# A hybrid decoder block on one core: one pool of 90 tiles in place of four pools, and a new written order

## The chip, the cores and the metric

The kernel runs on one core of one Trainium2 chip. The metric is the device time of one execution in microseconds (us). Five engines work side by side: PE (TensorE, the matmuls), DVE (VectorE), ACT (ScalarE), POOL (GpSimd) and SP (SyncE). SP and POOL compute nothing here: SP issues the loads and stores, POOL issues the DMAs that add into a tile on chip. "L284" is line 284 of the kernel.

## The reference, cut to what matters

One decoder layer on x of 512 tokens by 1024 columns, f32, with D_FF = 2816:

```python
mod = silu(c) @ ada_w + ada_b
shift1, scale1, gate1, shift2, scale2, gate2 = split(mod, 6)
h = rmsnorm(x, norm1_w) * (1 + scale1) + shift1
proj = h @ w_in                              # one projection, split into 14 column groups
...                                          # conv4 and silu on q, k, v
o_g = gated_delta_chunked(q_g, k_g, v_g, log_decay, beta)   # 4 heads, chunks of 64, triangular solve
o_g = rmsnorm(o_g, gdn_out_norm_w) * silu(gz)
o_n = nsa_attention(q_n, k_cmp, v_cmp, k_slc, vsl, k_win, vwn, gates)   # 4 heads, 3 branches
x = x + gate1 * (concatenate([o_g, o_n]) @ w_out)
h2 = rmsnorm(x, norm2_w) * (1 + scale2) + shift2
a, b = split(causal_dwconv(h2 @ ffn_w_up, ffn_conv_w, ffn_conv_b), 2)
x = x + gate2 * ((silu(a) * b) @ ffn_w_down)
```

## The kernel before, in words

**Products.** Every f32 product is made of three matmuls on fp32r halves. `split` (L337) rounds a tile to its high half with a copy on ACT or DVE and takes the low half with a subtraction on DVE; `split_acc` (L341) writes minus the high half on ACT or DVE and lets a POOL DMA add the source to it (`accum_op`), which spares DVE. The up and the down projection of the MLP use a seven-product scheme on 256-token halves (`pair`, L1211, and L1285 to L1370): sums and differences of weight blocks are formed by DVE adds and by more accumulating DMAs on POOL.

**Stages.** The modulation vectors (`adat`, column sums on DVE, L459), the first projection columns (`g0`), the convolution and the chunked delta rule of four heads, the compressed, selected and sliding attention, the output projection, the gates (`gate_b`, L932 to L936, which loads `adag`), the up projection (`wu`) and the down projection (`wd`). The triangular solve goes through DRAM: blocks are stored to `du`, stepped through on DVE in 64 rows, stored to `dx`, and loaded back as four tiles.

**Order.** The Python code only records operations: `_Plan.record` (L234) appends each one, `either` records one that may run on ACT or on DVE. `ORDER` and `CHOICE` are packed tables; `order()` (L247) gives the one order in which all operations are written and the engine of each `either`. Within each engine the instructions run in that order, each as soon as its inputs are there. SP's queue is such an order too: a DMA whose tile slot is not yet free holds up every DMA written behind it.

**Slots.** `emit` (L257) gives a tile its slot when its first operation is written: the slot that has been free the longest in its class. It is handed back after the operation written last on that tile. What is loaded into a slot therefore waits for that earlier tile's last reader. The classes (L295): S 74 tiles of 512 columns, W 8 (high and low halves of weights), R 4 of 1024 (weights as they are loaded), A 4 (the `adat` and `adag` loads), s 32 small ones, P the 8 PSUM banks. C holds tiles that stay for the whole run, each at its own place: parameters `pt`, constants `ct` (1219 columns), `ident`, the state `St`. All instructions of the plan are issued in `emit`, so their line is L284. A warm-up of 59 matmuls on the identity precedes the work.

Of the kernel before, what the change touches and what calls it, by code (L numbers as in the profile page):

```python
# [62 lines left out]
c-oy?cbrV;*FWdZ%r-  # L63
<>y@cpi?<H6wT1W&xf&|e8Nwg?I)C36<L??v=(S_)%{Se6#qIc1ITWp)T&w0PkbMK6m*Za@=na|GLd!Ksx_nhZ$6b<o?@{9@iJ(H3WB|74MQgafqh~3X
p@lrebMe5Kt2_sMF`TzIxiusPhUoN^S%cKoil%M_-r!^bRqF%UOEJ|8adh+ACB0Z4%@>B{^I9-
v4l9|rnX*~*~1Gs)H|CRrHwKr+Kr2Tt~*5U7tJeJaQNa{x%OgbtBD4Om|26}>d(qqgMDM=@!KAn=Q@&)}QNfMBkC|UfVKOJ2Z8yv|*8PGE){wBDq52Ab
0((o%umYZjT>9*uU|8$ffg}~ErJPV^oas#a%d=zGS89eYyidk7dsYQpyZ`#ADB%Q;U#}bKEGooKOJ(Zi1A1!{#O7p<Ei;|HVfeYbg2R^J9j@Emi=mz%C
i)`%pka^~OB0)t_$g(|VWL*Cxg8MAAovSFOBiKz2x+|Hm$4Jt9Qqq@}$R*LVdg!4<({*{BPD>2tKPOLcA47F%x7-
mA_TNf|Q7v#U3_UZ@HH<$mwP}x(r2=$Ge&ymS2Aocj2&zPJatouMNO5qwB<OevyUvDnbAgHkDF%HQM9aXJ3{*+BnbnKaJnD>9>xRcCI~>o5{dp)+j$+>
)DnUtdPoglMK?74h`W^ecF6A)mdU?-  # L70
# [1443 lines left out]
```

## Time and profile before

| | before |
|---|---|
| three runs, us | 665.75, 666.3, 668.78 (median 666.3) |
| profiled execution: its own time, us | 668.34 |
| profiled execution: span, us | 666.6 |
| instructions in the profile | 12647 |
| matmul records | 4177 |
| mean granted TensorE clock | 0.997 |
| DMA, MB | 129.39 |

The profile is of one execution, whose span begins with its first instruction; 1.7 us of its time lie around the span. All times inside the run are counted from the start of the span. PE is the TensorE matmul stream, PEld its weight loads, which run beside it. In a row of the timeline "[0.98 <-DVE S]" means that the engine stood idle for 0.98 us just before, and that an instruction of DVE that wrote an S tile ended the wait. "S<-dx" is a load from the DRAM tensor `dx` into an S tile; SPq and POOLq are the DMA-issuing parts of SP and POOL. The granted clock is at full speed in the whole run, so it plays no part below.

### The profile page before, as it was taken

The numbers are of one execution on the slowest core, as the hardware profiler recorded it, in microseconds if no ns is written. First come the engines' busy times: TensorE is split into PE (matmuls) and PEld (weight loads), VectorE is DVE, ScalarE is ACT, GpSimd is POOL, SyncE is SP. The second block draws the span as 40 slices with busy tenths as digits, with TensorE's granted clock in tenths as the row PEclk, the third lists the DMA queues.
The fourth block names the chain that finished last, engine by engine and source line by source line (L and its number), as shares of the span: only waits on it lengthen the run. The fifth ranks groups of instructions, "written<-read, shape, count | busy, mean of one in ns | idle before, by whom it ended". The sixth has DMA issues, their size and how long they took to land.

```text
span 666.6 us, 12647 instructions
## 1 busy us (share of the span) xinstructions
PE 655.7 (98%) x4177; PEld 586.0 (88%) x4177; DVE 627.6 (94%) x1541; ACT 464.9 (70%) x1157; POOL 126.9 (19%) x148
## 2 busy tenths in 40 slices
PE   8999999999999999999999999999999999999997
PEld 8887788888888878888999999999999997877885
DVE  7999999997899999889999999988999998999997
ACT  7655895645579999656786557576668788987740
POOL 0000000111000004300123244323333432245100
PEclk9999999999999999999999999999999999999999
DMA  9985436666652659965877799898999999999703
GB/s 322 392 306 187 170 134 211 196 158 130 219 162 76 215 176 227 220 198 155 252 175 160 181 181 218 165 198 161 196 224 197 217 233 250 220 217 201 141 0 127
DMA packets 65321, 129.39 MB, mean 194 GB/s; under 512 B 11092, under 2 KB 11620, under 8 KB 65256
## 3 DMA queue, kind: packets, MB, share of 16 engines
q1 hardware_dynamic: 44632, 91.07, 40.7%
q0 software_dynamic: 20624, 37.52, 34.2%
q8 instruction: 33, 0.54, 0.3%
q14 instruction: 32, 0.26, 0.1%
HBM read 108.11 MB, written 3.41 MB: 167 GB/s over the span
## 4 chain that ended last, share of the span: by engine, by line
PE 79%; DMA 8%; DVE 6%; ACT 4%; issue 2%; SPq 1%; ACTq 0%; DVEq 0%
PE P L284 79%; DVE S L284 4%; DMA S<-in_wd_dram 4%; ACT S L284 3%; DMA R<-in_wu_dram 2%; ACT W L284 1%; DVE W L284 1%; DMA S<-in_adat_dram 1%; DMA A<-in_adat_dram 1%; DMA S<-dx 1%; SPq L284 1%; DVE s L284 0%; ACT R L284 0%; ACTq L284 0%; DVEq L284 0%
## 5 line engine op out<-in xcount | busy, mean ns | idle before, releaser
L284 PE MATMUL P<-S,W 128*128 128x256 f32 (+1 forms) x2037 | 304.2, 302 | 1.6 <-ACT S L284 1.0
L284 PEld LDWEIGHTS P<-S,W 128*128 128x128 f32 x2037 | 272.3, 191 | 15.6 <-ACT S L284 1.6
L284 PE MATMUL P<-W,S 128*128 128x512 f32 (+2 forms) x722 | 188.1, 395 | 0.7 <-DVE W L284 0.5
L284 PE MATMUL P<-S,S 128*128 128x512 f32 (+4 forms) x864 | 175.8, 323 | 1.3 <-DVE S L284 1.3
L284 PEld LDWEIGHTS P<-W,S 128*128 128x128 f32 (+1 forms) x722 | 131.0, 186 | 29.1 <-DVE W L284 2.4
L284 PEld LDWEIGHTS P<-S,S 128*128 128x128 f32 (+2 forms) x864 | 132.6, 188 | 16.8 <-ACT S L284 1.4
L284 DVE TENSOR_TENSOR S<-S,S 128x256 fp32r<-128x256 f32 (+16 forms) x318 | 140.9, 474 | 4.8 <-ACT S L284 1.5
L284 ACT ACTIVATE W<-S 128x512 fp32r<-128x512 f32 x149 | 91.4, 625 | 38.9 <-PE P L284 26.1
L284 ACT ACTIVATE S<-P 128x256 f32<-128x256 f32 (+5 forms) x200 | 78.9, 419 | 50.2 <-PE P L284 47.3
L284 DVE TENSOR_TENSOR W<-S,W 128x512 fp32r<-128x512 f32 x155 | 104.5, 684 | 6.3 <-ACT W L284 3.7
L284 ACT ACTIVATE S<-S 128x256 fp32r<-128x256 f32 (+3 forms) x198 | 91.0, 491 | 27.8 <-DVE S L284 22.6
L284 POOL DMA_DIRECT2D S<-R x45 | 41.8, 1016 | 306.3 <-ACT S L284 200.9
L284 ACT ACTIVATE W<-R 128x512 fp32r<-128x512 f32 (+2 forms) x115 | 64.4, 575 | 27.6 <-PE P L284 23.0
L284 POOL DMA_DIRECT2D S<-in_wu_dram x63 | 56.8, 937 | 136.2 <-DVE W L284 125.0
L284 DVE TENSOR_TENSOR S<-P,S 128x256 f32<-128x256 f32 (+3 forms) x116 | 60.7, 528 | 4.1 <-ACT S L284 1.8
L284 DVE SCALAR_TENSOR_TENSOR S<-S,C,S 128x511 f32<-128x511 f32 (+1 forms) x84 | 62.3, 745 | 1.1 <-ACT S L284 0.5
L284 DVE TENSOR_TENSOR W<-R,W 128x512 fp32r<-128x512 f32 (+2 forms) x103 | 59.6, 590 | 1.1 <-PE P L284 0.6
L284 PE MATMUL P<-C,S 128*128 128x128 f32 (+3 forms) x345 | 56.5, 272 | 0.4 <-DMA S<-in_adat_dram 0.3
L284 PEld LDWEIGHTS P<-C,S 128*128 128x128 f32 (+2 forms) x345 | 43.8, 155 | 7.9 <-ACT S L284 1.0
L284 ACT ACTIVATE S<-S,C 128x512 f32<-128x512 f32 (+1 forms) x63 | 42.0, 675 | 7.0 <-DVE S L284 6.2
L284 ACT ACTIVATE S<-S,s 128x128 f32<-128x128 f32 (+4 forms) x78 | 36.3, 485 | 1.1 <-PE P L284 0.5
L284 ACT ACTIVATE S<-R 128x512 fp32r<-128x512 f32 x48 | 29.4, 627 | 10.5 <-DMA R<-in_wu_dram 5.8
(96 smaller groups left out, 502.7 us busy)
## 6 DMA issues: line engine op xcount, KB each, us to landing
S<-in_wu_dram POOLq DMA_DIRECT2D x63, 256.0 KB, 5.2
R<-in_wu_dram SPq DMA_DIRECT2D x23, 512.0 KB
S<-R POOLq DMA_DIRECT2D x45, 256.0 KB, 5.1
S<-in_wu_dram SPq DMA_DIRECT2D x42, 256.0 KB
S<-in_wd_dram SPq DMA_DIRECT2D x40, 256.0 KB
S<-in_adat_dram SPq DMA_DIRECT2D x32, 256.0 KB
A<-in_adag_dram SPq DMA_DIRECT2D x32, 256.0 KB
A<-in_adat_dram SPq DMA_DIRECT2D x32, 256.0 KB
```

The source lines that it names most:

```text
L284: getattr(engines[eng], method)(*map(place, args), **{k: place(v) for k, v in kw.items()})
```

## The change

**One pool.** W and A disappear; their tiles come from S, which grows from 74 to 90. The constants `ct` become three S tiles of 512 columns, loaded by three DMAs in place of one, and `St` becomes an S tile, so their slots can be handed on when they are last read. 74 + 8 + 4 + 3 + 1 = 90, so the space on chip is the same but for the 317 columns by which three tiles exceed the constants. R, s, P and the other C tiles stay. In the constants' layout "bd", "row0" and "win" move behind "cmask", so that no constant straddles two tiles.

**New tables.** `ORDER` and `CHOICE` are new. The operations are the same but for the two more DMAs of the constants: 3985 written for PE, 1476 for DVE, 1016 for ACT and 144 for POOL in both, and 321 DMAs on SP before, 323 after. 90 `either` operations go from ACT to DVE and 90 the other way. ACT's table loads, which are put in where its function changes, go from 7 to 11. Matmuls and weight loads that wait on a semaphore: 751 before, 625 after.

Where rows are shown, a name is the tile's class, its number in the plan and, behind the underscore, the number of the instruction in the written program at which the tile is first used. Tile numbers are higher by 2 after the change, because of the three `ct` tiles: S440 before is S442 after. What stands in brackets are the semaphores that the instruction waits for.

First place: SP's queue around the loads that bring the solved blocks back from `dx` (S386, S411, S469, S440 before). Before:

```order
L284 DMA dx_82<-S384_91 64x512 [waits DVE_49]
L284 DMA A705_2021<-in_adat_dram 128x512 [waits DMAHW1_49,DVE_49]
L284 DMA A716_2028<-in_adat_dram 128x512 [waits DMAHW2_49,DVE_49]
L284 DMA S386_2036<-dx_82 128x4x32 [waits DMAHW6_49,DMAHW3_49,DMAHW0_49]
L284 DMA A727_2040<-in_adat_dram 128x512 [waits DMAHW4_49,DVE_49]
L284 DMA S411_2055<-dx_82 128x4x32 [waits DMAHW5_49,DVE_49,PE_49]
L284 DMA S469_2088<-dx_82 128x4x32 [waits DMAHW3_49,DVE_49]
L284 DMA A718_2116<-in_adat_dram 128x512 [waits DMAHW7_49]
L284 DMA S440_2162<-dx_82 128x4x32 [waits DVE_49]
L284 DMA A784_2228<-in_adat_dram 128x512 [waits DMAHW1_49]
```

The same place of SP's queue after the change (S388, S413, S471, S442):

```order
L281 DMA dx_76<-S386_83 64x512 [waits DMAHW1_49,DVE_49]
L281 DMA S388_1977<-dx_76 128x4x32 [waits DMAHW3_49,DMAHW2_49,DMAHW1_49]
L281 DMA S781_1982<-in_adat_dram 128x512 [waits DVE_49]
L281 DMA S751_1989<-in_adat_dram 128x512 [waits DMAHW4_49,DVE_49]
L281 DMA S413_2015<-dx_76 128x4x32 [waits DMAHW5_49,DVE_49]
L281 DMA S471_2027<-dx_76 128x4x32 [waits DMAHW7_49,DMAHW6_49,DVE_49]
L281 DMA S442_2045<-dx_76 128x4x32 [waits PE_49,Activation_49]
```

The four loads now stand within 69 instructions of each other (1977 to 2045) where they stood within 127 (2036 to 2162), and the last of them is written ahead of the `adat` loads that it stood behind.

DVE's rows around the reader of the fourth of these tiles. Before, the reader is the row that names S440, the product with a mask:

```order
L284 TENSOR_TENSOR S470_2150<-S469_2088,C1_874 128x512
L284 TENSOR_TENSOR S395_2169<-P394_2154,C1_874 128x512
L284 TENSOR_TENSOR S441_2173<-S440_2162,C1_874 128x512
L284 TENSOR_SCALAR S521_2159<-S521_2159,s530_2083 128x128
L284 TENSOR_TENSOR S415_2179<-P414_2125,C1_874 128x512
```

After, it is the row that names S442:

```order
L281 TENSOR_TENSOR C332_2166<-C331_1392,C306_1471 128x16
L281 SCALAR_TENSOR_TENSOR s532_2136<-s533_2138,s532_2136 128x16
L281 SCALAR_TENSOR_TENSOR s533_2138<-s532_2136 128x16
L281 TENSOR_TENSOR S443_2173<-S442_2045,S4_1051 128x512
L281 TENSOR_TENSOR s533_2138<-s533_2138,s531_2134 128x16
L281 SCALAR_TENSOR_TENSOR S708_2178,s706_2177<-S707_1313,S17_221 128x512
```

The reader's own tile is first used at instruction 2173 in both programs; the load stood 11 instructions ahead of it (2162) and now stands 128 ahead (2045).

Second place: SP's queue where the loads of the down weights begin. Before:

```order
L284 DMA R1650_7281<-in_wu_dram 128x1024 [waits DMAHW4_49,DMASW1_49]
L284 DMA S1652_7290<-in_wu_dram 128x512 [waits DMASW2_49,DMAHW5_49,DVE_49,Activation_49]
L284 DMA R1984_7434<-in_wd_dram 128x1024 [waits DMAHW6_49,DMASW5_49,DVE_49]
L284 DMA S1805_7474<-in_wd_dram 128x512 [waits DMAHW7_49,DMASW2_49,DVE_49]
L284 DMA S1723_7536<-in_wd_dram 128x512 [waits DMAHW0_49,PE_49]
L284 DMA S1735_7542<-in_wd_dram 128x512 [waits DMAHW1_49,PE_49]
L284 DMA S1809_7563<-in_wd_dram 128x512 [waits DMAHW2_49,PE_49]
L284 DMA S1719_7593<-in_wd_dram 128x512 [waits DMAHW3_49,DVE_49,Activation_49]
L284 DMA S1743_7595<-in_wd_dram 128x512 [waits DMASW5_49,DMAHW4_49,DVE_49,Activation_49]
```

After:

```order
L281 DMA R1652_7236<-in_wu_dram 128x1024 [waits DMAHW7_49,DMASW2_49,DVE_49]
L281 DMA S1725_7261<-in_wd_dram 128x512 [waits DMAHW0_49,PE_49]
L281 DMA S1737_7282<-in_wd_dram 128x512 [waits DMAHW1_49,PE_49]
L281 DMA R1986_7417<-in_wd_dram 128x1024 [waits DMASW6_49,DMAHW2_49,DVE_49,Activation_49]
L281 DMA S1771_7424<-in_wd_dram 128x512 [waits DMAHW3_49,PE_49]
L281 DMA S1721_7428<-in_wd_dram 128x512 [waits DMAHW4_49,PE_49]
L281 DMA S1729_7575<-in_wd_dram 128x512 [waits DMAHW5_49,DMASW5_49,DVE_49]
L281 DMA S1807_7579<-in_wd_dram 128x512 [waits DMAHW6_49,PE_49]
L281 DMA S1733_7581<-in_wd_dram 128x512 [waits DMAHW7_49,PE_49]
```

The first loads of `wd` stand further ahead: S1723 moves from instruction 7536 to 7261 (as S1725) and S1719 from 7593 to 7428 (as S1721), while the add that reads S1723 first is row 1215 of DVE before and row 1214 after.

The diff, cut to its core (of the tables one line each, the whole of the rest but for repeated edits of one form):

```diff
-NCST = _fill(CST, [("triu", 128), ("ones", 128), ("negT", 128), ("neg", 128),
-                   ("lv", 2 * 128), ("bd", 4), ("eye16", 256), ("cmask", 4 * 32), ("row0", 1), ("win", 2 * NCMP)])
+NCST = _fill(CST, [("triu", 128), ("ones", 128), ("negT", 128), ("neg", 128), ("lv", 2 * 128), ("eye16", 256),
+                   ("cmask", 4 * 32), ("bd", 4), ("row0", 1), ("win", 2 * NCMP)])
...
-c-oy?cbrV;*FWdZ%r-
+c-oD72bdJa^LEwD-t7gBbYzYoASW3_kerktQKDi%5F{xeAQBAtBcli+DCs~Xi6Ek64iH6@=pi{MNK}w~z=hqJuK(LTd&{9d&-
...
-    sizes = {"S": (74, 512), "W": (8, 512), "R": (4, 1024), "A": (4, 512), "s": (32, 32), "P": (8, 512)}
-    pools = {c: ctx.enter_context(tc.tile_pool(name=f"p_{c}", bufs=1)) for c in ("C", "S", "W", "R", "A", "s")}
+    sizes = {"S": (90, 512), "R": (4, 1024), "s": (32, 32), "P": (8, 512)}
+    pools = {c: ctx.enter_context(tc.tile_pool(name=f"p_{c}", bufs=1)) for c in ("C", "S", "R", "s")}
...
-    def load_w(src, cls="W", acc=False):
+    def load_w(src, acc=False):
...
-            hi, lo = plan.tile(cls, (P, m), F32R, "w"), plan.tile("S" if acc else cls, (P, m), F32R, "w")
+            hi, lo = (plan.tile("S", (P, m), F32R, "w") for _ in range(2))
...
-    pt, ct, ident = keep("pt", NPAR), keep("ct", NCST), keep("ident", P)
+    pt, ident = keep("pt", NPAR), keep("ident", P)
+    ct = [u("ct") for _ in range(3)]
...
-        return ct[:, at + a:at + a + (m - a if n is None else n)]
+        return ct[at // 512][:, at % 512 + a:at % 512 + a + (m - a if n is None else n)]
...
-            raw = plan.tile("S" if i < 2 else "A", (P, 512))
+            raw = plan.tile("S", (P, 512))
...
-    Q.dma_start(ct, cst)
+    for i, c in enumerate(ct):
+        Q.dma_start(c[:, :min(512, NCST - 512 * i)], cst[:, 512 * i:min(NCST, 512 * i + 512)])
...
-    St = keep("St", 512)
+    St = u("St")
...
-                raw = plan.tile("A", (P, 512))
+                raw = plan.tile("S", (P, 512))
...
-        w = plan.tile("W", (P, 512), F32R, "w"), u("wl", F32R) if acc else plan.tile("W", (P, 512), F32R, "w")
+        w = plan.tile("S", (P, 512), F32R, "w"), u("wl", F32R) if acc else plan.tile("S", (P, 512), F32R, "w")
```

More of the change, by code (lines that the diff above doesn't have):

```diff
@@ new lines @@
+Xq1?Ci{RcXf4jg}1tUV<_Ms<9uWfblwd{Qw#c9+LJ|JNoQhw)<{q~(M{PZ&*AAyi7;>f|2`GNcctj4FcrYv-
+{$uVd5xw^Pr8k#s8F5H<vsMXO8#F|J5z2tB;`=Qv*A*IcSsSsC#6xk5$#9Q7+l|_?YLf&ob)K|6CcG<Je`v`DoQ=+P0`$)m3y)eckSsLjQIxc?t;b{DN
+lcjBZcUyY!k1H>AaMomuaD7N)9~b#5YwIqD2qGQ+{fU>voxxjr);wO8iuu{FH%TCFkW4Pzgv;yzxUGHkHTkHI$u_7?kIwD-ua%z{3Uf<p&>$bW4={4xT
+lY+~B7eBoq)mel1f!MPt<I;K)bEL8k+*x6#6nF^-
+j5n9Ca&ha(q7_xKn^Pzt0`fNXH*qL;n$I6Z`Wn+`}7TrbFX(vAv~$T@k4($Npo30w<PH`$DtD@^Oash+P4X-
+J!;5!x)|XVgU*C^PAfq=BpQC{4hqm|`eX{sgy7x#$;ZO_gXT?hit`Q5b0g>cwFOm<r+gCNyq8B%(+Agv_P-XtNPKT$Q@?qcp*|7-MBaF+cq-
@@ new lines @@
+Nsff8t(dN7uAx%xPQvD9AZDIblpY|*y&~->gt$zgra4o)dppKttRrU%CKhyPlDfhzQ2RpAlVc*$@hzFar;@f5o=-
+)i@yj|v~yFk+tS+MMA{GP>@@Y6U7dn%32V1ggqMgOOHS%Yy<M#(Pg*6d({4^W1S>aMC__yv9bNLmLM<9<Fbn36d#NaR%oJySM3>+~OXCg9k*T|olDHCP
+(v`h#9cwz!w2nmUqz&D|Oznh5Fx9kj({5QWb-
+1WpgiMp&Le`bgJZkS))H*Fw4KjfA@fjdBR4wakAOL;0AKWRPE=!GPsbTp+G0EN+=tOPpE$&{F?t<2RC6-
+m)@o4VhT51~R96YLi(GxNX&@29z(!8=|Jd4KgX!WNo#|ZnVB(AE?Sp(#4WEHVQst~yIYWjUD=*VH~Me{t#-
+tTCXu$^0=|N2%HXDd&&TTn(Y)@b9y*6(hreM4qC?_(sxkqe|qW$UOL#w%88_<p)QO68#;Qb20Rqapm2VA=Gln;5EbT<+M3YPwXkHp)<EC3jIJtn;qcbh
@@ new lines @@
+b{pBh@6%Z<ST4#=|mwXmyrVRE#UDoT{+#)xCMP`U`WE-
+$JBw3tObliS`n&>x@BtXuTkP{NJW!ik{znRv94YfcpceiFldPL8%Iiu7KRzSnJ#qT!hN<6^y^RwL*4CX-MESm%(*{^^q)sj#s8-
+*2T!BK$r*INwD<q&{tRbR0>csH%Gm?>Ht5gR&ghItiLdhq0y32kY96p^E~yFjI%bmcM<b7DsP79(o}7<dPoJ8DL=^*K!aODo-
+r>te*>)@E=<>4hc5zOkEfon>{Mx^T3H+1gP>5w%!g&ND2CVGt=_Ubt9v0kepAK*D^yb}t$4|+{FZ|}%A!OS2h21aqq!sXLvygpjf0ihs-
+2~Mj^f>}MqNMCO}8*gwRC@HTUkWbQ*u*XmZx~8Dg(>7$wf^JyYBuW?V)XLa9^C(OR6-
+4R?kMhlIHH`v+z<o=!LL1JHs9lUmvkNxWxDdjqNJaPSohb^?4&5b`DD%=Ch<KWiL_9wJiYU91=a=-
@@ new lines @@
+r!>0$OJIbH3T=kMTyat)a9eLd?&#!X?J&ihtL8UIR=tkI}rWj?ed5u5NPcO@9FOG6Wb(AN#X_Qk^k&`Wv=hQH3po--
+&@DYwm;Y8I>ZXuho=xs>zM_BtS(B#6tP=rS|SI{2s-k=gv+&Uo^bk&ujW;MrWYWOHcVpVbLf|1opr-
+(0x^_oB@os+1ku%dWK<e0M{!b6lZQ7?^Cr3Q7;YYNKZ3DDun^c%G3o|Kkcu(i6*+tzXGkVLDwI#Pr4ZpLS<q~)pwFH?Gy{Wy<&AU&bqB>njvyFl=5`+d
+xBB-tiY@o=?9Or@MG?b>PEC}-q?3Gx@|tQav+>ARj`4V+9Pkoz!ImlWiB+XBsuBuXK2S;%H{Q!9?5fix5R%*E3Vo)~Q5+eZz|*j9@-
+56x%?V%YbxLM`(pWwh|cL4#A!A}=SwZjOuA03Sa`Yq*`#Qe2?^271=fVhbo71J}8zyIG<85qSL*Shl9Vj@rmN+7M_O5mbLtg7}z?-
+yh;`=Jkm06{)fu#y1gmQ_`KtOVkH^Qkw8gDS;l>n@p;euO(V-
@@ new lines @@
+xisyAZ?U*KY_bBqfm|u4$pUrmz7rln-%XK;xb~M0CRe%tsV7>87gGsX&|aAuJv8ktyqypomEPF2t7>YkrjLzmF3>@4<2DM-
+U1MPTB<S2>Q`QxFqSszlA@9hdUIZ<CsJld7%+}|c(1`0&ZQQMmZkq-NMptlO8v5P?(t7D1sLEUMI1d!zs0iKxYV~FK12vHEm@H|s(UGjrJ7#6SsM)oNr
+|Z-
+ZoUIL)7NY~I8?<Yjyf1H=wco#iA`gV}b?BX(hp&EH^d7(oZObZ&rx@y|!hM{VKcbj=r0aW6=9m2A)1yp{Te1RWAEf^##Z2k+aH|Wrn;A90v}(eq<QJJt
+)0DS2h)5KbRj+n>O?r=JnSIB9W6gMEZ83;x?X=dSP2KdLalMi5?I9kO-
+{gjPxF7+#m|%E#L+?;U)uG<$9*r_)cMd3$Ced5rdHY<|;OSC<kEzdT4(_WP+h_U$GOCK0eoH*PxGS7(E$VkX)q^cOh4{NlRbU-
+m?{oX8(I%6zbAP4r)hsF?O^jWBY-$YS40mR>x$A?HdooS*idzFjoP~zJYf?-
@@ new lines @@
+07@W;!Z*HIA;YBkNC9lv(VY9CpN7qd3OO<z__dBFvnDQO}ko0L$8IbK!V2(o2yh29%UIS9zrZfs-SZZnTYJuYhm^TZEX-
+0Sko;Ldsef1ulyO5{KSBQ=AG*Fh%O}u{=-
+>RIZUP7k%FtBjEY4b4+@XyRREsNw;()%$Uy?gFqt8<ucQO*lX|H9Z(u`suv$;%o;s#}yt9%l~a`?W)*+6(C4n(`yBQB}AOG<~MbM^<{8%AjPse_=)s|J
+Rwbog3C>wbsm${@hm6p(`UYB5AB2vd+*W-
+fLC}Tl(u|{N!(&F%@&!#q9iEGi`cFVIC*irjJU+2lViOSrHs$R)U`)2R77O^xEzac?5pxgmpni0Bal!kMo+F*VemGM~t_dB)il*R0GJeDXoxiOsz^hOO
+itM7eI#_hgxnk@0ytVg+P1#q&Qzt+JhE{O*IMaD|nx^>N8NOFCU>5RPF)$StWf#qtdGsDKZGwF_XPayaRbVgD>D$$D<CILvKHp&5D4&{|!+pO=67=a>(
@@ new lines @@
+#g#QFur_(%rC3ma%#XuRX+08eH$8W)A`s_zLn1N@<FK9P(;lqt!?`J3v5&Gp}`-
+7%4(SB!@xcNw)aP1L1ieP)e$&TuYv2;xfHnvU${|PhE8?p9HJLjkab*1`bjIydcII=FABWDJyio_#$_l!?^aW3f~rVQ+V85Izym$ym_F|%$7ut#LhVZS
+lTP;jbJHmJV4dac2yyqj!TN8>PazaDQ5@u>+D^4T?qPkBM&qTCw4E%>Sv$QtnT=voyMyVWCm&Hdd*26-
+Iml!`>v*gB090Opw6d?<X&h5GZ0(DXH7qjLb_QeJ2Tf>#xmk)@8g=fGS_WUQhpgHg9M(*BnJmN0gXS74_xaH$6&k@uwlwbp<d+Hju&U0JC5gUNL+#gG&
+odw<Qw;QHC^GER#tI$@>*!dztm2LJMjOA`S|T~9+M5*vhbjY0Bm&7#0dF=<vs_pElg=2!^YHke%TQ#h*Cn4m>CJbPhmEyv+}963Pmni^E$0+(7vLjE;X
@@ new lines @@
+yoOFLACj3)lRK9s{y*FBFMSY5&J)dCM6-CUCl454nV#+;Ft7hT_CGT1_^Hm4@H30dYXSii~`50@HVqd-nUD1<kKElXO<dir@$s$U=|lh>@j$cU9ukSCI
+ZXmq<gTh4&bDXdY!y;Xb$w_7mR5*a>Pq!z2&x9)A2#pcQCdmAnl2wwQnzU<Q8T-
+hKI@lTCH>zl?Kb`0@OPObCDzDyW7(Q#7><@j5G3k!>k~ULp(VEdDJ$T!K<4HN&gOs`Vf-`gx}_+AY~{YtUOIcBG-vAF*64+)<L;OJuvew=3V=(NNR8LG
+H)Ny54)Q$FT<zLP=1r+C4;Bi@;;D9QMQ49f@-
+@w3w^PvAWu~}po{BFhId|mln;>wti?>slhMYu?xLSxMQ8pafbfSxYpaAX$U(?iOU;oK_%cr)_5UQILz-
+5K_dvQXa`qPHzco*oHLU*dsVBuTxngukiz8vH{pfvp-tg~(R>v9LaEvYZ%zZR%lV6DBf>dCyw;={Em=cOngW%@^Dh@Jp)ns{{^%>0oyv7cFjzt!V-
@@ L189 @@
-aNhmL~;&7
+c-muNfPnxOMg~%V11^aMBGtix08~`~36>B59156Xj0_?`n;IOT90-Py5J!73u;6tlir1K+E>vKGc>)F?mM>@k8O!0(F*%J<!T=`6%7o-
+QY~JHQ7hu9A!2pji7IXoqj~Wo73JeJh2VgP+U?;*uf&*r{0;+ie*j&d5brc6wPXp8fCPa)mpa%t7s!+g@Zdibj0}=I1Bu07z++r3ysfQ6gTv1)*z(8cW
+MoFd$U`ugiAOPjJ5&-
 """
@@ L1117, in hybrid_block @@
     plan.sect = "wo"
-    wos = [load_w(wo[k], "S", True) for k in range(KT)]
+    wos = [load_w(wo[k], True) for k in range(KT)]
     for t in range(NT):
@@ L1151, in hybrid_block @@
     EARLY = 1
-    held = {(f, s): (load_w(wu[f, s], "S"), bank("up")) for f in range(EARLY) for s in range(2)}
+    held = {(f, s): (load_w(wu[f, s]), bank("up")) for f in range(EARLY) for s in range(2)}
     for a in (0, 256):
```

199 lines of the change are left out of this document (73 added, 126 removed).

## The prediction

> **What bounds it now.** I read the page's first line, then PE's idle time along the run, then the chain of waits for what stands behind it.
>
> ```profile
> PE 655.7 (98%) x4177; PEld 586.0 (88%) x4177; DVE 627.6 (94%) x1541; ACT 464.9 (70%) x1157; POOL 126.9 (19%) x148
> ```
>
> PE is the bound, and its work does not change (as many matmuls of the same shapes). What an order can win is PE's idle time: 666.6 - 655.7 = 10.9 us. The windows (busy time of PE, PEld, DVE, ACT, POOL, then clock and DMA share) say what a matmul costs when it is fed:
>
> ```profile
> 100.00:165.00 65.00, 65.00 (x334) 55.02 (x332) 59.31 (x172) 36.13 (x100) 6.94 (x8) 1.00 0.66 174
> 330.00:440.00 110.00, 110.00 (x915) 109.76 (x914) 107.27 (x206) 74.14 (x154) 35.35 (x41) 1.00 0.85 181
> 470.00:535.00 65.00, 65.00 (x543) 65.00 (x543) 63.62 (x119) 45.24 (x87) 24.00 (x27) 1.00 0.98 207
> 612.00:660.00 48.00, 48.00 (x216) 39.71 (x215) 47.65 (x94) 25.50 (x55) 4.49 (x5) 1.00 0.41 95
> ```
>
> 110.00 / 915 = 0.120 us for 256 columns, 48.00 / 216 = 0.222 us for 512. DVE is nearly full there as well, which becomes a rival. The chain of waits (start, length, what) passes through these loads after the start-up:
>
> ```profile
> 161.68 5.72 DMA S<-dx
> 173.16 5.74 DMA A<-in_adat_dram
> 441.85 5.87 DMA R<-in_wu_dram
> 460.56 5.84 DMA R<-in_wu_dram
> 535.45 5.83 DMA S<-in_wd_dram
> 553.66 6.57 DMA S<-in_wd_dram
> 579.81 6.78 DMA S<-in_wd_dram
> 599.54 5.97 DMA S<-in_wd_dram
> ```
>
> A load takes 5.7 to 6.8 us from issue to landing. Behind each of the eight PE stands idle (PE's timeline: start, length, tiles, count, idle before and who ended it):
>
> ```profile
> 169.38 0.79 PE L284 MATMUL P<-S,S 128*128 128x128 f32 x5 [0.98 <-DVE S L284]
> 180.97 0.49 PE L284 MATMUL P<-S,S 128*128 128x128 f32 x2 [0.28 <-DVE S L284]
> 449.21 0.62 PE L284 MATMUL P<-S,W 128*128 128x256 f32 x3 [0.27 <-ACT W L284]
> 450.00 0.39 PE L284 MATMUL P<-S,W 128*128 128x256 f32 x1 [0.17 <-ACT S L284]
> 467.47 0.50 PE L284 MATMUL P<-S,W 128*128 128x256 f32 x2 [0.61 <-ACT S L284]
> 541.74 0.40 PE L284 MATMUL P<-S,W 128*128 128x256 f32 x2
> 542.32 0.50 PE L284 MATMUL P<-S,W 128*128 128x256 f32 x2 [0.18 <-ACT S L284]
> 561.74 0.50 PE L284 MATMUL P<-W,S 128*128 128x512 f32 x1 [0.22 <-DVE W L284]
> 591.85 0.50 PE L284 MATMUL P<-W,S 128*128 128x512 f32 x1 [0.28 <-DVE W L284]
> 609.37 0.50 PE L284 MATMUL P<-W,S 128*128 128x512 f32 x1 [0.21 <-ACT S L284]
> ```
>
> The rows name DVE or ACT because they split what was loaded; their own rows name the load (two of them):
>
> ```profile
> 167.42 0.69 DVE L284 TENSOR_TENSOR S<-S,C 128x512 f32<-128x512 f32 x1 [1.48 <-DMA S<-dx]
> 560.33 0.63 ACT L284 ACTIVATE W<-S 128x512 fp32r<-128x512 f32 x1 [1.82 <-DMA S<-in_wd_dram]
> ```
>
> **The change, part by part.**
>
> *The eight waits on loads.* The nine idle entries add up to 0.98 + 0.28 + 0.27 + 0.17 + 0.61 + 0.18 + 0.22 + 0.28 + 0.21 = 3.2 us. The rows hide a little more, since the end of a matmul is modelled: from 541.74 to 542.32 pass 0.58 us for two matmuls of 0.120, 0.34 lost where 0.18 is shown; from 449.21 to 450.00 pass 0.79 for three, 0.43 lost where 0.17 is shown. So 0.16 to 0.26 each is hidden; I take 0.2, 1.8 for nine, and 5.0 us in all (4.6 to 5.5). Does the new order free them? I call "lead" the PE time of the matmuls written between the place where a load can be issued at the earliest (its slot handed back, SP's queue ahead of it served) and its first reader, counted on the two orders at the prices above. The last `dx` load (S440, now S442) goes from 3.0 to 12.2 us; the `adat` loads A705 and A779 from about 3 to over 18; of `wd`, S1723 from 4.7 to 26.8, S1743 4.0 to 16.2, S1785 4.9 to 11.6, S1837 5.0 to 10.2, S1859 and S1867 4.8 to 11.6 and 10.7. Against landings of 5.7 to 6.8 all were short, and all are clear now. In `wu`, R1442 goes from 4.6 to 9.0 and R1494 from 5.8 to 9.5, but R1468 from 4.9 only to 5.0: R still has four tiles, and I keep its wait, the two entries at 449 and 450, 0.27 + 0.17 + 2 x 0.2 = 0.8. Removed: 5.0 - 0.8 = 4.2 us. If the freed waits come back as waits on DVE, nothing is removed.
>
> Here the Trainium skill speaks against the change. Its page "DMA: Bandwidth & Descriptors", section "Anatomy of one DMA — SWDGE (gpsimd) path", puts one DMA at about 2.0 us and its bytes at 436 GB/s, a fit for POOL's path: 256 KB would land after 2.6 us, an estimate from that page. By that figure leads of 4 to 5 us were long enough, and this term would be 0. The trace does not agree: 5.7 to 6.8 us on SP's queue.
>
> *Other waits of PE on ACT and DVE.* PE's idle 10.9 us hold 4.6 after the last matmul (below), 1.2 ahead of the first, 1.0 at start-up rows shown below and the 3.2 above: 0.9 is left, some seven short waits, 2.3 us with 0.2 hidden in each. The new order writes fewer results just ahead of their reader: 288 instead of 412 stand within 0.7 us of PE time of it. That third of 2.3 is 0.8; bounds 0 and 2.3.
>
> *Four more table loads on ACT.*
>
> ```profile
> L284 ACT ACT_TABLE_LOAD x7 | 9.0, 1283 | 0.8 <-PEq L1504 0.7
> 50.00:100.00 50.00, 49.67 (x248) 39.21 (x247) 48.24 (x112) 40.17 (x132) 0.00 (x0) 1.00 0.47 164
> ```
>
> 4 x 1.283 = 5.1 us of ACT, between 50 and 165 us of the run. What hides them is ACT's idle time there, 50.0 - 40.17 = 9.8 and 65.0 - 36.13 = 28.9 us. With that cover it costs nothing, without it 5.1; I take one visible wait of 0.3, as in the row at 542.32 with its hidden part.
>
> *Start-up and constants.*
>
> ```profile
> 7.47 0.35 PE L284 MATMUL P<-C,C 128*128 128x128 f32 x1 [0.73 <-DMA C<-in_ide_dram]
> 11.54 0.27 PE L284 MATMUL P<-C,S 128*128 128x1 f32 x1 [0.28 <-DMA S<-in_adat_dram]
> q1 hardware_dynamic: 2010, 3.93, 104.2%
> ```
>
> The last row is the DMA share from 10 to 20 us: the engines are full, and the first fourteen loads are the same ones in a slightly different row (the identity third, not sixth). The bytes set the end, so 0, with 1 us either way for who waits first. Two more constant loads on SP lie behind these, with nothing queued behind them that is due at once: 0.
>
> *The end.* DVE works on without a gap past PE's last matmul:
>
> ```profile
> 660.62 1.32 PE L284 MATMUL P<-W,S 128*128 128x512 f32 x8
> 662.00 0.69 DVE L284 TENSOR_TENSOR S<-S,S 128x512 f32<-128x512 f32 x1
> 662.60 0.42 DVE L284 TENSOR_TENSOR S<-P,S 128x256 f32<-128x256 f32 x1
> 663.06 0.42 DVE L284 TENSOR_TENSOR S<-S,S 128x256 f32<-128x256 f32 x1
> ```
>
> 666.6 - 661.94 = 4.6 us lie behind the last matmul. Before, DVE's last split stands 38 matmuls ahead of the end, 18 DVE instructions behind it. After, three are read by the matmuls that are the 28th, 26th and 22nd from the end, and 16 DVE instructions are written behind the last of them, the one that the 28th reads. 12 of these at 0.60 to 0.61 (662.00 to 662.60) and four at 0.42 are 9.0 us, against 28 x 0.222 = 6.2 us of PE. If DVE brings this split just in time, the end is 9.0 - 6.2 = 2.8 us behind PE instead of 663.48 - 661.94 = 1.5: +1.3. If it comes early, 0; if DVE is behind by more, up to 3. I take +0.4.
>
> Sum: -4.2 - 0.8 + 0.3 + 0 + 0.4 = -4.3 us on the profiled execution, 668.34 to 664.0. That execution lies 2.0 above the median of the three runs (666.3), so the forecast is 662.0. With each term at its better end (5.5 - 0.8 of loads, 2.3, 0, 1 and 0) it is 658.3; at the worse ones that I hold for likely (loads 3.2, less R1468's 0.8, the others 0, tables 0, start 1, end 1.3) it is 666.2.
>
> **The rivals.**
>
> *No change, 665.5 (0.22).* DVE becomes the bound where PE's waits go: in the two long stages of the MLP it has 110.00 - 107.27 = 2.7 and 65.00 - 63.62 = 1.4 us to spare, 2%, and PE has no idle entry there at all. Of the 4.2 us, 2.5 lie at 467 us and later, in stages of that kind; if DVE cannot go faster they come back. -4.2 + 2.5 = -1.7, and with the tables' 0.3 and the end's 0.4 and no other wait gone it is -1.0; I take -0.8, since the end is then likelier late. Against it: waits as the 1.48 above are DVE's own idle time, and go with the loads.
>
> *Slower, 670.5 (0.12).* The accumulating DMAs of POOL land late, since SP's loads, issued sooner, share the engines with them.
>
> ```profile
> S<-in_wd_dram POOLq DMA_DIRECT2D x8, 256.0 KB, 8.8
> q0 software_dynamic: 1066, 1.95, 76.8%
> q1 hardware_dynamic: 498, 0.89, 16.0%
> S<-in_wd_dram POOLq DMA_DIRECT2D x3, 256.0 KB, 5.7
> q0 software_dynamic: 3002, 5.46, 51.8%
> q1 hardware_dynamic: 4832, 8.82, 45.8%
> ```
>
> The first three rows are 595 to 612 us, the others 535 to 595. In the new order two of the `wd` accumulates have leads of 8.4 and 8.9. If SP's queue takes a share as in the second stretch, POOL's falls from 76.8 to 51.8%, and 8.8 us become 13: 4.4 too late at each of the two, 8.8 in all, -4.3 + 8.8 = +4.5, which is 670.8, or 670.5 with 0.3 of it covered. It decides from a landing of 8.7 us. Against it: in the second stretch, with the larger share for SP, POOL's landed in 5.7. The Trainium skill's same page, section "Queues, rings and completion order", has each engine take turns between the queues by packets; that allows the rival, and the two landings do not bear it out.
>
> *More, 657.5 (0.10).* All the load waits go at their upper price, R1468's with them, all the other short waits, and the start comes a us earlier: -5.5 - 2.3 - 1 = -8.8, and 668.34 - 8.8 - 2.0 = 657.5. For it: nearly every load's lead grows. Against it: the first loads move as many bytes as before.
>
> **How the numbers follow.** Forecast 0.56, no change 0.22, slower 0.12, more 0.10. About 0.5%, 3.3 us, can be told from no change here (the three runs span 665.75 to 668.78): faster is below 663.0, slower above 669.6. The forecast's own range is 658.3 to 666.2, and with its weight about 662.0 two thirds of it lie below 663.0: 0.38; with "more" that is 0.48. Same: 0.18 + 0.22 = 0.40. Slower 0.12. The range reaches from 657.0 to 668.0: it holds the forecast's two bounds and the no-change case with 1.7 us above the median for the spread of the runs, and leaves out the slower case and up to half of the larger gain, 0.17.
>
> **What would show it.** Right: no `dx`, `adat` or `wd` load on the chain of waits after the start-up; DVE's idle entries of 1.48 and ACT's of 1.82 gone; an `in_wu` load into R still on the chain near 445 us; PE idle near 8 us in place of 10.9 (2.4 shown of the loads, 0.5 of the others). Wrong: the same loads still on the chain, with the same landings; PE idle entries released by POOL's DMAs in the down stage (the slower rival); DVE without a gap and PE with gaps after 467 us (no change); table loads ahead of PE's waits between 50 and 165 us; a tail of over 6 us behind the last matmul.

## The result and the profile after

Over nine executions each the median goes from 666.77 to 661.07 us; the ratio is 0.9922, with a 95% interval from 0.9899 to 0.9945. The change is faster by 5.7 us, and the forecast was 662.0. The two profiled executions lie further apart, 668.34 and 661.06, since that of before was one of its longer ones. One of the executions reported below, of a_only with 710.21 us at a granted clock of 0.849, was in a slower state and is left out of its row.

PE's line of the page after, in the columns of the one shown of before:

```profile
PE 651.9 (99%) x4177; PEld 586.6 (89%) x4177; DVE 626.8 (95%) x1540; ACT 468.5 (71%) x1162; POOL 126.5 (19%) x148
```

The span is 659.0, so PE is idle for 7.1 us where it was 10.9. The two stretches of the MLP that held six of the eight late loads, in the windows view of before (busy time and instructions of PE, PEld, DVE, ACT, POOL, then clock, DMA share and GB/s):

```profile
433.00:533.00 100.00, 98.95 (x818) 98.27 (x818) 94.55 (x174) 69.92 (x131) 36.16 (x41) 1.00 0.93 199
533.00:616.00 83.00, 82.09 (x428) 68.62 (x427) 79.52 (x172) 70.87 (x156) 29.71 (x34) 1.00 0.97 224
```

And after:

```profile
433.00:533.00 100.00, 100.00 (x836) 100.00 (x835) 96.98 (x180) 71.19 (x136) 34.83 (x40) 1.00 0.95 209
533.00:616.00 83.00, 83.00 (x419) 70.92 (x418) 82.75 (x181) 71.20 (x152) 30.66 (x35) 1.00 0.96 216
```

PE has no idle time left in either. In the first 18 more matmuls pass in the same 100 us, and 18 x 0.120 is 2.2 us: that is twice the 1.05 us that PE stood idle by its busy time. What a late load costs is more than the idle entries show, so from here on I measure PE's loss otherwise: the time from one matmul's start to the next one's, less the price of the first by its columns (0.227 us for 512, 0.120 for 256, 0.110 for 128, 0.07 to 0.11 below), summed over a stretch. By stretch of the span, in us, from the traces, each cell rounded by itself:

| run | 0-33 | 33-150 | 150-183 | 183-330 | 330-433 | 433-533 | 533-616 | from 616 | all |
|---|---|---|---|---|---|---|---|---|---|
| before | 4.5 | 2.3 | 2.1 | 3.1 | 0.1 | 2.0 | 3.4 | 0.0 | 17.5 |
| after | 3.5 | 2.2 | 0.5 | 2.1 | 0.0 | 0.0 | 0.0 | 1.4 | 9.5 |

After 33 us, PE's timeline has two idle entries left (start, length, tiles, count, idle before):

```profile
84.38 0.96 PE L281 MATMUL P<-S,S 128*128 128x512 f32 x3 [0.21 <-ACT S L281]
623.22 2.12 PE L281 MATMUL P<-S,S 128*128 128x512 f32 x8 [0.39 <-DVE S L281]
```

The second is new. The chain of waits leads from it to the only load that is on the chain (start, length, what). After the change the chain can be followed back only to 605.81 us, so of the stages before that it says nothing; for them the idle entries and the table above have to do. ACT's timeline and the DMA view from 606 to 621 us say what the load met:

```profile
612.64 8.15 DMA S<-in_wd_dram
623.22 30.03 PE P L281 x132
```

```profile
620.87 1.77 ACT L281 ACTIVATE S<-S 128x512 fp32r<-128x512 f32 x4 [3.26 <-DMA S<-in_wd_dram]
```

```profile
q0 software_dynamic: 966, 1.76, 72.2%
q1 hardware_dynamic: 144, 0.26, 6.1%
S<-in_wd_dram POOLq DMA_DIRECT2D x6, 256.0 KB, 8.3
```

It is the last `wd` load into an S tile (S1881). In the new order it stands right ahead of its split with a lead of 6.6 us, while six accumulating DMAs of POOL that were issued from 608 us on have most of the engines' time (72.2% for POOL's queue, 6.1% for SP's). It took 8.15 us and cost PE 1.35.

The four more table loads are there, and 33 to 150 us, where they fall, lost no more than before:

```profile
L281 ACT ACT_TABLE_LOAD x11 | 14.1, 1283 | 2.3 <-DVE s L281 1.4 <-PEq L1503 0.7
```

At the end DVE now waits for PE, by 0.19 us, where it lagged:

```profile
653.27 0.69 DVE L281 TENSOR_TENSOR S<-P,S 128x512 f32<-128x512 f32 x1 [0.19 <-PE P L281]
655.06 0.42 DVE L281 TENSOR_TENSOR S<-S,S 128x256 f32<-128x256 f32 x1
```

### The profile page after: what moved, and what is told of

It reads as the page before. It is cut to its first block, busy times and chain, and to the rows that moved or that the text cites. A ratio compares the mean times of both kernels' runs of the same rounds, so it can differ in the third digit from the quotient of the medians.

```text
span 659.0 us, 12614 instructions
## 1 busy us (share of the span) xinstructions
PE 651.9 (99%) x4177; PEld 586.6 (89%) x4177; DVE 626.8 (95%) x1540; ACT 468.5 (71%) x1162; POOL 126.5 (19%) x148
## 5 line engine op out<-in xcount | busy, mean ns | idle before, releaser
L281 PE MATMUL P<-S,S 128*128 128x256 f32 (+5 forms) x3687 | 608.9, 324 | 0.7 <-DVE S L281 0.4
L281 PEld LDWEIGHTS P<-S,S 128*128 128x128 f32 (+3 forms) x3687 | 524.5, 190 | 54.8 <-DVE S L281 1.7
L281 DVE TENSOR_TENSOR S<-S,S 128x512 fp32r<-128x512 f32 (+12 forms) x477 | 240.4, 545 | 5.7 <-ACT S L281 2.2
L281 ACT ACTIVATE S<-S 128x512 fp32r<-128x512 f32 (+3 forms) x345 | 173.6, 548 | 53.2 <-DVE S L281 28.8
L281 ACT ACTIVATE S<-P 128x256 f32<-128x256 f32 (+4 forms) x197 | 79.2, 420 | 55.1 <-PE P L281 52.4
L281 ACT ACTIVATE S<-R 128x512 fp32r<-128x512 f32 (+2 forms) x161 | 90.4, 587 | 20.4 <-PE P L281 10.2
L281 DVE SCALAR_TENSOR_TENSOR S<-S,C,S 128x511 f32<-128x511 f32 (+2 forms) x112 | 81.8, 744 | 0.8 <-ACT S L281 0.2
L281 DVE TENSOR_TENSOR S<-R,S 128x512 fp32r<-128x512 f32 (+2 forms) x107 | 62.3, 594 | 1.0 <-ACT S L281 0.5
L281 PEld LDWEIGHTS P<-C,S 128*128 128x128 f32 (+1 forms) x285 | 36.6, 145 | 7.7 <-issue 0.6
L281 DVE SCALAR_TENSOR_TENSOR S<-S,S 128x512 f32<-128x512 f32 x62 | 41.5, 685 | 0.6 <-PE P L281 0.5
L281 POOL DMA_DIRECT2D S<-S x20 | 17.5, 935 | 46.7 <-ACT S L281 42.7
```

The lines of the kernel that those rows point to most:

```text
L281: getattr(engines[eng], method)(*map(place, args), **{k: place(v) for k, v in kw.items()})
```

## The experiments

The tables of an order can't be read, so the edits of the order are given as lists of what is moved. "Lead" is counted as in the prediction. All runs, with the ratio to before and PE's loss as above:

| run | median us | ratio (interval) | 0-33 | 150-183 | 183-330 | 433-533 | 533-616 | from 616 |
|---|---|---|---|---|---|---|---|---|
| pool_only | 661.32 | 0.9932 (0.9909 to 0.9956) | 3.2 | 0.4 | 2.8 | 0.5 | 0.5 | 0.0 |
| pool_early | 661.84 | 0.9931 (0.9912 to 0.9949) | 4.2 | 0.3 | 3.5 | 0.9 | 0.7 | 0.0 |
| late7 | 664.98 | 0.9977 (0.9958 to 0.9995) | 6.9 | 0.4 | 2.1 | 0.0 | 3.6 | 1.6 |
| fix1 | 662.60 | 0.9929 (0.9901 to 0.9956) | 8.3 | 0.5 | 2.1 | 0.0 | 0.0 | 0.0 |
| fix1_again | 659.88 | 0.9905 (0.9880 to 0.9929) | 8.6 | 0.4 | 2.1 | 0.0 | 0.0 | 0.0 |
| w_only | 669.24 | 1.0036 (1.0019 to 1.0053) | 3.4 | 0.7 | 3.3 | 3.5 | 4.5 | 0.1 |
| a_only | 663.1 | 0.9934 (0.9916 to 0.9952) | 3.0 | 1.4 | 2.8 | 0.7 | 0.5 | 0.0 |
| c_only | 661.97 | 0.9895 (0.9864 to 0.9926) | 3.5 | 0.7 | 3.6 | 1.3 | 0.6 | 0.0 |
| ac_only | 663.53 | 0.9915 (0.9886 to 0.9945) | 3.7 | 1.1 | 3.2 | 1.7 | 0.2 | 0.0 |
| pool85 | 676.88 | 1.0146 (1.0130 to 1.0162) | 3.0 | 1.5 | 11.7 | 1.2 | 3.9 | 0.1 |
| fix1_warm | 660.08 | 0.9891 (0.9859 to 0.9922) | 2.5 | 0.4 | 2.1 | 0.0 | 0.0 | 0.0 |

The first column spreads by 6 us for a reason of its own, which the last experiment takes up. The others are what the order and the pools set: in them fix1 and fix1_again, the same program, agree to 0.1.

### The pool alone (pool_only)

```diff
-    sizes = {"S": (74, 512), "W": (8, 512), "R": (4, 1024), "A": (4, 512), "s": (32, 32), "P": (8, 512)}
+    sizes = {"S": (90, 512), "R": (4, 1024), "s": (32, 32), "P": (8, 512)}
 ORDER, CHOICE   # those of before, the two more constant loads written right behind the first
```

> The order and the engine choices of before in the one pool of 90 tiles. Counted on the order, the shortest lead of a wd load grows from 4.0 to 7.0 us by the pool alone, since a slot is handed back sooner; the last dx load gets 5.4, many adat loads stay at 3 to 5, the two R loads of wu at 4.6 and 4.9. Theory one (the late loads were the loss): the 3.4 us that PE lost between 533 and 616 us are gone, the 1.8 near 170 and the 2.0 between 433 and 483 stay, so about 663.4 (ratio 0.995). Theory two (the new order helps by its distances between ACT, DVE and PE, the loads do not matter): 666.8, nothing gone.

Measured 661.32, ratio 0.9932: all of the change's gain, with the order of before. In the windows the two stretches are fed but for 0.26 us:

```profile
433.00:533.00 100.00, 99.94 (x832) 99.69 (x831) 96.67 (x177) 70.01 (x135) 34.85 (x40) 1.00 0.94 209
533.00:616.00 83.00, 82.80 (x422) 70.68 (x421) 82.46 (x181) 71.80 (x164) 31.98 (x37) 1.00 0.99 227
```

More went than theory one gave: near 170 us and in `wu`, where the leads that I had counted (3 to 5.4 us) had hardly grown; why those waits shrank stays open. What theory two said, that the new order's distances help and the loads do not matter, falls: the order is the old one. The opposite part, the new order in the old pools, can't be tried: the new order needs all 90 tiles at once.

### Thirty loads earlier, in the pool (pool_early)

```diff
 ORDER   # of pool_only, 30 DMAs on SP written 5 to 100 operations earlier:
+        # 13 of adat, 2 of dx, 4 of adag, 11 of wd; each then has a lead of 8.8 us or more
```

> As the run with the pool alone, but 30 loads on SP (of adat, adag, dx and wd) are written earlier, so that each has a lead of 8.8 us or more; the rows of PE, DVE, ACT and POOL are those of before, in the order of before. The R loads of wu keep 4.6 and 4.9. Theory one: the losses near 170 us go as well, 666.8 - 3.4 - 1.8 = 661.6 (0.992), with the 2.0 between 433 and 483 us left. Theory two: 666.8.

Measured 661.84, no better than the pool alone. The time is what theory one gave, but the run does not bear it out, since the losses that the moves were to take away had gone with the pool. Leads of 7.0 us were enough for `wd`, and more brought nothing.

### Seven loads late again (late7)

```diff
 ORDER   # of the changed kernel, seven DMAs on SP written later:
-        # leads 12.2 (S442), 26.8, 16.2, 11.6, 10.2, 11.6, 10.7 us (S1725, S1745, S1787, S1839, S1861, S1869)
+        # leads  3.0 (S442),  4.8,  4.2,  5.0,  5.7,  5.0,  4.5 us, by 34 to 277 operations
```

> The changed kernel with seven loads written later (the last dx load and six of wd), so that their leads are 3.0 to 5.7 us as before the change; nothing else moves. Theory one: their waits come back, about 1.1 us near 165 and 3.4 between 533 and 616, so 661.1 + 4.5 = 665.6, with PE idle entries behind loads again. Theory two, or loads that land in under 4 us: 661.1.

Measured 664.98, 3.9 us longer than the changed kernel, with PE's waits back where the loads were put late:

```profile
554.80 5.42 PE L255 MATMUL P<-S,S 128*128 128x512 f32 x23 [1.23 <-ACT S L255]
592.21 33.04 PE L255 MATMUL P<-S,S 128*128 128x512 f32 x144 [0.41 <-DVE S L255]
```

```profile
550.72 0.63 ACT L255 ACTIVATE S<-S 128x512 fp32r<-128x512 f32 x1 [2.71 <-DMA S<-in_wd_dram]
```

Six loads of `wd` with leads of 4.2 to 5.7 cost 3.6 us between 533 and 616. Nothing but seven rows of SP stands elsewhere in the order, though 490 S tiles get another slot by it, since slots are handed out in turn. The waits that came back are named by the loads, so the price of the late loads is shown. The `dx` load with a lead of 3.0 cost nothing (0.4 from 150 to 183, as after): a short lead on the order is not yet a wait. The changed kernel shows the same for `wd`: counted in this way the load of S1799 has a lead of about 4.5 there, S1741 6.4 and S1845 6.6, and the stretch from 533 to 616 lost nothing.

### One load earlier (fix1, fix1_again)

```diff
 ORDER   # of the changed kernel
-        # load of S1881 two operations ahead of its split, lead 6.6 us
+        # load of S1881 98 operations ahead of its split, lead 14.8 us
```

> The changed kernel with one load written earlier: the last wd load into an S tile, which waited for its slot at 612.64 us and landed 8.15 us later; its lead goes from 6.6 to 14.8. Theory one: PE's loss of 1.35 us between 616 and 650 goes, 659.7 (0.998 of the changed kernel). If DVE is the bound there (36.0 of 38.0 us busy), it stays at 661.1 with the wait named by DVE alone.

> The changed kernel with the last wd load into S written earlier, once more for its time: in the first run PE's loss between 616 and 650 us was gone, but its profiled execution and two others ran the stretch from 12 to 24 us at half the clock. At a clock of 0.998 and more I expect 659.5 to 660.2, against 660.6 to 661.4 of the changed kernel.

PE's loss from 616 us on is gone in both. In 616 to 650 us PE is busy throughout, with 151 matmuls in place of 145, and 6 x 0.222 is 1.3 us. First after, then fix1:

```profile
616.00:650.00 34.00, 33.61 (x145) 26.68 (x145) 32.04 (x62) 10.96 (x26) 0.00 (x0) 1.00 0.18 43
```

```profile
616.00:650.00 34.00, 34.00 (x151) 28.16 (x150) 33.56 (x67) 12.97 (x30) 2.19 (x3) 1.00 0.29 55
```

Of the eleven executions six have a granted clock of 0.998 or more and take 659.47 to 660.23; seven of the changed kernel's nine have that and take 660.58 to 661.44. The middle ones are 659.7 and 661.1, so this load was worth 1.3 us. The other five have a clock of 0.991 to 0.995 and take 662.6 to 664.7; where along the run the clock fell is seen only in the two that were profiled.

### Which part of the pool (w_only, a_only, c_only, ac_only)

```diff
 # each with the order of before; the sizes of
-    S 74, W 8, A 4, constants and state apart
+    w_only:  S 82, A 4, constants and state apart
+    a_only:  S 78, W 8, constants and state apart
+    c_only:  S 78, W 8, A 4
+    ac_only: S 82, W 8
```

> Before, with the eight W tiles alone put into S (82 of S, A still 4, constants apart), order as before. Counted on the order the wd loads are as late as before (shortest lead 4.1 us, 13 under 6). If the leads of the loads are the whole matter, it stays at 666.8, or 666 with the last dx load (4.5 for 3.0). If the splits' wait for a W tile that PE still reads (ACT rows that write W waited 49.0 us for PE in the profile before) is what holds R tiles and so the next R load, the 2.0 us between 433 and 483 go and part of the rest: 664 or less.

> Before, with the four A tiles alone put into S (78 of S, W still 8), order as before. Counted on the order the shortest lead of a wd load grows from 4.0 to 6.9 us, those of adat stay or shrink (1.4 at the shortest), the R loads of wu stay. By the leads: the 3.4 us between 533 and 616 go, the 2.0 between 433 and 483 stay, 663.4. If the W tiles are the cause: 666.8.

> Before, with the constants (three tiles) and the state alone put into S (78 of S, W 8 and A 4 apart), order as before. From the time when the constants are last read, S has four tiles more, as in the run with A's tiles in S: the shortest wd lead is 6.9 us. If the number of tiles free in the late stages is the matter, the losses between 433 and 616 us fall as there (5.4 to about 1), and with the waits on A tiles near 170 us left it is 662 to 663.5. If it were A's sharing: 666.8.

> Before, with A's tiles, the constants and the state in S (82 of S) and only W's eight apart, order as before. By the number of free tiles: as the run with the pool alone, 661.3, perhaps 660.5, since W's tiles do not take turns with S's. If putting W into S is what the pool needs: 663 or more.

A's four tiles in S, or the constants' three and the state's one, bring 661.97 to 663.53; W's eight bring nothing, 669.24, with more loss in both stretches of the MLP than before (3.5 and 4.5 against 2.0 and 3.4). The windows of a_only and, behind it, of w_only:

```profile
433.00:533.00 100.00, 100.00 (x830) 99.56 (x830) 96.01 (x177) 71.13 (x134) 35.07 (x40) 1.00 0.95 205
533.00:616.00 83.00, 82.88 (x427) 70.87 (x426) 82.20 (x180) 73.34 (x163) 31.56 (x37) 1.00 1.00 233
```

```profile
433.00:533.00 100.00, 98.96 (x806) 97.21 (x806) 94.19 (x173) 68.39 (x129) 35.12 (x40) 1.00 0.91 196
533.00:616.00 83.00, 81.25 (x422) 67.63 (x421) 78.60 (x171) 69.59 (x153) 29.68 (x34) 1.00 0.95 221
```

So it is not the sharing, and the theory of the splits that wait for a W tile falls. A and the constants are tiles that stand unused in the late stages: A's are last read by the gates, the constants by the attention, and the MLP has from then on four or eight tiles more to load into. Counted on the order, the fewest S tiles that are free from `wu` on are 0 before, 4 in a_only and c_only, 8 in ac_only and in the pool alone. The shortest `wd` lead goes with it, 4.0, 6.9, 6.9, 7.9 and 7.0 us, and so does the loss from 533 to 616, 3.4, 0.5, 0.6, 0.2 and 0.5. From 433 to 533 it is less clear: the loss falls from 2.0 to between 0.5 and 1.7, although R still has four tiles there and the loads into R stand where they stood; that the splits get their S tiles sooner, and so hand R back sooner, is my reading and not shown. a_only, c_only and ac_only don't differ from the pool alone by more than their intervals, and no ranking of them is meant. The 663.53 of ac_only lies where I expected it if the pool needed W's tiles (663 or more), but the executions of before that were timed with it and with c_only were longer too, 668.86 in the median, and its ratio of 0.9915 can't be told from the 0.9932 of the pool alone. So whether W's tiles add anything is not shown. Why w_only is slower than before stays open.

### Five tiles fewer (pool85)

```diff
-    sizes = {"S": (90, 512), "R": (4, 1024), "s": (32, 32), "P": (8, 512)}
+    sizes = {"S": (85, 512), "R": (4, 1024), "s": (32, 32), "P": (8, 512)}
```

> The order of before in one pool of 85 tiles, five fewer than in the run with the pool alone and just as many as that order needs at once. The shortest lead of a wd load is 5.4 us instead of 7.0, four of them under 6. By the leads about 1 us of the 3.4 comes back between 533 and 616: 662.3 against 661.3. If it is the sharing and not the number of tiles: 661.3.

Measured 676.88: 15.6 us more than with 90 tiles and 10 more than before, against 1 that I expected. The late `wd` waits come back (3.9 us), but most of it is lost from 183 to 330 us, which I had left out of account. There the order needs all 85 tiles at times. The chain passes through loads again:

```profile
229.08 2.71 DMA S<-in_adat_dram
241.18 5.68 DMA R<-in_w_dram
```

```profile
248.48 0.69 PE L254 MATMUL P<-S,S 128*68 128x512 f32 x2 [2.64 <-DVE S L254]
```

From the landing of the first to the issue of the second DVE has no gap of more than 0.04 us, and from 237.9 to 241.2 SP issues two `adat` loads, one of `wu` and one of x as tiles come free, and behind them the compression weights (R) that PE needs next. Whether SP's queue or the R tile's own readers held that load the views don't tell apart. What the run does show is that the number of tiles above what the order needs at once is what pays here, not the sharing by itself. That holds for the order of before: the new order needs all 90 at once and is no slower, since it spends the spare tiles on earlier loads.

### The start (fix1_warm)

```diff
-IDLE = 59
+IDLE = 72        # 13 more warm-up matmuls, whose result nothing reads, behind the 39th
```

> The changed kernel with the last wd load into S written earlier, and 13 more warm-up matmuls (72 for 59, 13 x 0.120 = 1.56 us) written behind the 39th, where PE stood idle for 1.2 to 1.5 us at 11 us in the executions that then ran at half the granted clock until 22 us. If that idle time sets the clock, every execution has a clock of 0.998 or more and takes 659.5 to 660.4, with none near 664. If the clock falls for another reason, a third of the executions still takes 664 to 665. If the warm-up delays the work behind it, all are longer by up to 0.6.

Measured 660.08, all six executions between 659.73 and 661.4, two of them above the 660.4 that I expected at the most, and all with a clock of 0.998 or more. In the profiled execution of fix1_again PE stood idle at 11 us, and the clock then fell:

```profile
11.38 0.38 PE L255 MATMUL P<-C,S 128*128 128x1 f32 x2 [1.49 <-DMA S<-in_adat_dram]
```

```profile
12.00:16.00 4.00, 4.00 (x20) 4.00 (x21) 3.10 (x15) 3.74 (x9) 0.00 (x0) 0.51 1.06 400
20.00:24.00 4.00, 4.00 (x27) 4.00 (x26) 3.98 (x15) 3.08 (x6) 0.00 (x0) 0.71 1.04 391
```

With the longer warm-up there is no idle entry in the profiled execution, and the clock holds:

```profile
12.00:16.00 4.00, 4.00 (x37) 4.00 (x38) 2.82 (x13) 2.94 (x9) 0.00 (x0) 1.00 1.06 404
```

That the idle time is the cause is not shown by this. Nine of the thirty executions with the shorter warm-up and the same start (2 of 9 of the changed kernel, 2 of 10 of late7, 5 of 11 of fix1 and fix1_again) have a clock of 0.995 or less; at that rate six in a row would be free of it by chance about one time in eight. And ac_only stood idle for 0.80 us a little later, and its clock did not fall:

```profile
12.22 0.38 PE L254 MATMUL P<-C,S 128*128 128x1 f32 x2 [0.80 <-DMA S<-in_adat_dram]
12.00:16.00 4.00, 3.78 (x34) 3.78 (x35) 3.59 (x17) 3.91 (x10) 0.00 (x0) 1.00 1.05 385
```

This kernel is 6.9 us under the executions of before that were timed with it (666.96), and 1.0 under the changed kernel's median.

## Why the prediction was right, and where it was not

**The load waits** were the gain, as forecast: 2.1 + 2.0 + 3.4 = 7.5 us of loss in their three stretches became 0.5. The term was too small, 4.2 for 7.0. Two steps of it failed. The hidden part per entry was not 0.2 but about 0.4, (7.5 - 0.5 - 3.2) / 9: behind a late load the matmuls that follow start a little late too, each by less than an idle entry shows. And the wait of R1468 (R1470 after the change), 0.8, did not stay: its lead of 5.0 us, counted on PE's work, was 8.1 in the trace (issued at 433.7, read by DVE at 441.8), since DVE reaches a row later than where it is written. So all the load waits went, as the rival "more" had it, and at more than its price of 5.5; the time stayed near the forecast because the new late load and the end took 1.8 back, and by luck, which the sum below tells.

**What frees them** I put down to the order's leads without telling order and pool apart. The pool alone does it. The new order with one load mended is worth 1.6 us on top (661.3 to 659.7, by four executions against six at full clock, whose times do not overlap); with its own late load, 0.2, which these runs can't tell from nothing.

**The load that it made late** was not forecast. I set leads against landings of 5.7 to 6.8 us and did not look for the ones that were 6 to 7 in the new order. S1881's 6.6 met a landing of 8.15; others as short cost nothing, as said under late7. By the shares of the two queues it is the mechanism of my slower rival turned about: POOL's accumulates held up SP's load, not the reverse. That is a reading, since no run changed the accumulates alone. It costs 1.35 us once, and the rival's price of 8.8 did not arise, since POOL's `wd` accumulates, 8.3 in the median there, held up next to nothing: no wait of PE or DVE names them, and of ACT's 3.4 us of waits on `wd` loads 3.26 are S1881's.

**The page's figure.** The Trainium skill, "DMA: Bandwidth & Descriptors", "Anatomy of one DMA — SWDGE (gpsimd) path", gives the fit from which I estimated 2.6 us for 256 KB, and I wrote that the trace does not agree. That was too wide. Where the DMA engines have time to spare, it agrees, on SP's queue too. These are chain entries of a_only and of w_only, with the engines' share at 0.60 (168 to 171 us) and 0.55 (204 to 207.1 us):

```profile
168.10 2.63 DMA S<-in_adat_dram
```

```profile
204.39 2.65 DMA A<-in_adat_dram
```

At the sites of the waits, with the engines' share at 0.95 to 1.02, it was 5.7 to 8.15, and late7 shows that leads of 4.2 to 5.7 are too short there. The size did not set it: of the prediction's eight, the `dx` load is 64 KB and took 5.72, the two into R are 512 KB and took 5.84 and 5.87, and the others are 256 KB.

**Other waits** (-0.8): 2.3 + 3.1 became 2.2 + 2.1, so -1.1. Near the size by luck: before shows three idle entries there (0.21, 0.29, 0.17) where I took some seven, and more loss hidden behind them than 0.2 each. **Table loads** (+0.3): nothing is seen of them; ACT's idle time covered all 5.1 us. **Start** (0): -1.0 between these two executions, by the clock: in that of before it was 0.81 and 0.76 from 12 to 20 us, in that of after 1.00. So the clock was not at full speed in the whole run of before, as the section on its profile has it. The first of the two windows:

```profile
12.00:16.00 4.00, 4.00 (x32) 4.00 (x32) 3.67 (x15) 3.78 (x9) 0.00 (x0) 0.81 1.05 397
```

Over all executions the new start is the worse one, which the medians hide: nine of thirty have a clock of 0.995 or less with it, and one of the 49 of before whose clock is on record. In the three of the nine that were profiled the fall lies at the start. In the changed kernel they are the two at 664.69 and 664.88 us, some 3.7 above the rest.

**End** (+0.4): from PE's last matmul to the end it is 659.0 - 653.97 = 5.0 us instead of 4.6, the size that I gave for another reason. DVE came early enough, with 1.5 us from PE's last matmul to its own end (653.97 to 655.48) as before (661.94 to 663.48); what is longer is the way from DVE's last add to the end of the span, 3.5 for 3.1.

**The sum** on the profiled executions was -4.3 and is -7.3: 7.0 + 1.1 + 1.0 gained, 1.35 + 0.4 lost, which makes 7.35 and differs by less than 0.1. The medians moved by only 5.7, which is nearer to the forecast than the working deserves: the sum was made against an execution 1.6 us above its median, about 1.0 of it the clock, and I took that difference off as a constant.

**No change** by a full DVE fell: with the loads in time DVE was busy for 82.75 of 83.00 us and PE for all of it, with no wait of PE on DVE.

## What to carry to other kernels

Count, by stage, the tiles that a class holds and nobody uses: here eight tiles of constants and early loads, put into one pool with the eight of the weights, were worth 5.5 us, most of it in the MLP (loss of PE 5.4 to 1.0), long after their last reader. Five tiles fewer than that cost 15.6, most of it in an earlier stage where the order needs all of them. Count a load's lead from the moment when its slot is handed back and SP's queue ahead of it is served, and set it against the landing in that stage, with the accumulating DMAs in flight: 7 us was enough for `wd`, 6.6 beside six accumulates was not, and leads of 4 to 7 were late in some places and not in others. A merged pool or a new order is worth a look at every load that it leaves right ahead of its reader.

## What the hardware showed that I had not expected

The granted clock fell early in some executions, and which ones goes with PE's idle time only in part. In the three profiled ones with 1.21 to 1.49 us idle at 11 us it was 0.50 to 0.59 from 12 to 20 us, and in two of them 0.71 and 0.73 from 20 to 24, which cost up to 5 us. With 0.28 and 0.47 idle at that place, in before and in pool_early, it was about 0.8 for 8 us; with none, or 0.19, it stayed at 1.00. But it also stayed at 1.00 with 0.36 at 11.3 us in a_only, with 0.80 at 12.22 us in ac_only and with 1.48 at 8.15 us in c_only, so these runs give no limit. After 13 more warm-up matmuls none of six executions showed it, where nine of thirty had; that is too few to be sure.

A load of 256 KB landed in 2.6 to 2.7 us where the DMA engines' share was 0.54 to 0.60, and in up to 8.15 beside six accumulating DMAs.
